# Hybrid encoder block on one core: gate of the product pairs one product later, dilated steps reordered, units run ahead

## The chip, the cores and the metric

The kernel runs on one core of a Trainium2 chip. The metric is the device time of one execution in microseconds; the median of the runs counts. The engines are named as the profile names them: PE (matrix engine; PEld is its weight load), DVE (vector), ACT (scalar), POOL (GpSimd) and SP (the sync engine, which here only issues DMAs). Each engine takes its instructions in the order in which the program wrote them to its queue, and each instruction waits until what it needs is done.

## The reference

One layer, one sequence of 1024 tokens of width 1024, float32. Three mixers run side by side on the normalised input: dilated window attention in three groups (A), grouped-query attention (B), and attention into a memory (M). Each is multiplied by a SiLU gate and projected; the three are merged by sigmoid gates and projected once more.

```python
h = rms_norm(x, g_pre)
a_qkv, bq, bk, bv, mq, ga, gb, gm, mg = split(h @ w_in)
aq, ak, av = rope(q of a_qkv), rope(k of a_qkv), v of a_qkv
for gi, (window, dil) in enumerate(((128, 1), (512, 4), (2048, 16))):      # 8 heads each, head size 64
    o_g, lse_g = dilated_window_attention(aq, ak, av of group gi, window, dil)
wts = softmax(stack(lses), axis=0)                                         # over the three groups
oa  = sum_g wts[g] * outs[g]
ob  = grouped-query attention of bq, bk, bv;   om = attention of mq into the memory
ya = (oa * silu(ga)) @ w_br_a;  yb = (ob * silu(gb)) @ w_br_b;  ym = (om * silu(gm)) @ w_br_m
gates  = sigmoid(mg + b_merge)
merged = gates[0] * ya + gates[1] * yb + gates[2] * ym
out = x + rms_norm(merged @ w_out, g_post)
```

## The kernel before

Every float32 matrix product is made of three products of a high and a low part (hh*wh, hl*wh, hh*wl); `split` makes the parts, ACT the high one (L105) and DVE the low one by a subtraction (L106). Nearly all the order after the grouped attention is written by hand: the text of the program is the order of each engine's queue.

**Start to 578.8 us.** Input norm, grouped attention, the projections that it needs, the values. The diff touches nothing here.

**The pairs (578.8 to 1081).** The remaining columns of the input projection are computed as 25 pairs of column blocks (`PAIRS`): in turn queries or keys that get their rotation ("rope"), and columns of the SiLU gates ("gate") or the merge gates ("merge"); the last is a merge pair. Each pair takes seven products of half size, after Strassen's scheme, of twelve matmuls each (`pair_product`, L1292), named A11, A12, S2, A22, S1, S3 and S4 by their operand. A product ends in a PSUM bank; `keep_copy` (ACT, L1296) copies some of them to SBUF, `c_add` adds two, and `c_fin` finishes a quarter of the result: a DVE multiplication by the row norm (L1098), then, in a merge pair, a tanh on ACT (L1106) and a store through ACT's own DMA queue into `thd` (L1107); in a gate pair a tanh (L1101), a DVE step and a store into `g2d` through SP. `k_block` splits the next operand, `turn_it` (POOL) rotates and `k_store` writes queries and keys.

**The turn (1081 to 1097).** `op_load`, `op_mult` and `op_split` fetch the first operand of the branch projections in two token halves (lo, hi), multiply it by its gate and split it into `hh` and `hl`.

**The dilated attention (1097 to 1300).** Twelve items, one for each pair of heads p (0 to 3) and group g (0 to 2), with eight steps T each. `plan` writes the order: in a step stand `trans` (PE turns the probabilities, DVE copies them out, L1555 and L1580), `soft` (DVE subtraction, ACT exponential L1542), a piece of the combination (`combining`), and loads or splits (`tokens`). `weave` puts between these steps, by costs, the pieces of a second stream: units 0 to 15 of the branch projections (`add_y`, L1815), 24 matmuls each, in two halves with a PSUM tile "d" of two buffers; `y_evac` empties one (DVE multiplies, L1344, POOL adds, L1345), `y_split` splits its weight, `y_load` and `th_load` fetch weight and merge gate.

`combine` joins the three groups of a head pair: fetch the statistics from memory (`cpt`, L1730), weights (DVE, from `cmn` L1735 to `ceg` L1746, with one ACT exponential L1739), write them to memory (put, L1751), read them back broadcast to the partitions (get, L1725), multiply and add the three outputs (`weigh`, L1760 and L1762; on POOL, for p = 3 the products on DVE), store. `STEP_T` gives the step of each piece. `b_load` and `b_split` fetch and split the grouped attention's output, the operand of units 8 to 15. `dl_load`, `dl_mult` (DVE, L1798) and `dl_split` fetch a combined head pair, multiply it by its gate and split it into `hh[k]`, `hl[k]`, the operand of units 16 to 23. All these loads are issued by SP.

**The ending (1300 to 1338).** After the last item, `ending` lists the pieces for p = 3 with their costs for `weave`.

**The y units 16 to 23 (1338 to 1382)**, `y_unit`, 24 matmuls each (L125), emptied whole (128x1024); between them stand the splits of the output weights (`LATER`) and of the merged result (`a_half`).

**The output projection (1382 to 1467)** and the final norm.

## Time and profile before

| | us |
|---|---|
| runs | 1469.06, 1469.36, 1475.54 |
| median | 1469.36 |
| profiled execution, its time | 1468.72 |
| its span in the trace | 1466.9 |
| PE busy | 1388.7 |
| DVE busy | 1028.3 |
| ACT busy | 659.9 |
| POOL busy | 600.4 |

How to read the lines that follow: in a timeline a line gives start, length, engine, source line of the program, operation, output<-input, shape and in brackets the idle time of the engine before the instruction and what ended it. In a table of waits a line gives engine, tile and line that waited, what it waited for, and then the microseconds in total, the number of times and the longest. In a table of windows each line gives the stretch, its length, the busy time of each engine, the granted clock of PE as a share of full speed, the busy share of the DMA engines and GB/s. SPq and ACTq are DMA issues on the queues of SP and ACT. Line numbers are those of the kernel before.

### The profile page before, as it was taken

What the parts mean: (1) busy time and instruction counts of PE and PEld (TensorE: products, weight loads), DVE (VectorE), ACT (ScalarE), POOL (GpSimd) and SP (SyncE); (2) the same over time, 40 slices, a digit from 0 to 9 for tenths busy, and PEclk for the clock granted to TensorE, in tenths of its full rate; (3) what the DMA queues carried; (4) which work ended last, traced back from release to release, by engine and by line L of the source; (5) the groups of instructions that cost most, each with busy time, mean ns of one, the idle gap of its engine ahead of it and who ended that gap; (6) DMA issues with size and microseconds to landing.
All of it is one profiled execution on the core that took longest, in us unless ns stands there. A gap on an engine that the chain in (4) does not pass through costs nothing.

```text
span 1466.9 us, 21800 instructions
## 1 busy us (share of the span) xinstructions
PE 1388.7 (95%) x7768; PEld 1109.3 (76%) x7768; DVE 1028.3 (70%) x1797; ACT 659.9 (45%) x1378; POOL 600.4 (41%) x455
## 2 busy tenths in 40 slices
PE   7999999999999999999999999999989899786997
PEld 7799986666666889887777788777767677565886
DVE  7768578677763987677766666677665655548977
ACT  6544366666554453333333333333346566432332
POOL 1416604676654002445455444555401325534303
PEclk9999999999999999999999999999999999888999
DMA  6347432232203795242333333333365667646454
GB/s 234 102 158 255 143 116 96 79 98 89 73 25 125 239 285 170 68 144 83 105 115 101 105 111 115 114 109 94 126 235 174 178 211 203 169 150 185 150 214 172
DMA packets 121341, 209.74 MB, mean 143 GB/s; under 512 B 33616, under 2 KB 62096, under 8 KB 121232
## 3 DMA queue, kind: packets, MB, share of 16 engines
q1 hardware_dynamic: 111920, 194.42, 41.5%
q10 hardware_dynamic: 9312, 13.93, 2.6%
q8 instruction: 61, 1.00, 0.3%
q14 instruction: 48, 0.39, 0.1%
HBM read 143.97 MB, written 64.32 MB: 142 GB/s over the span
## 4 chain that ended last, share of the span: by engine, by line
PE 70%; DVE 11%; issue 6%; ACT 4%; DMA 4%; POOL 3%; SPq 1%; ACTq 0%; DVEq 0%; POOLq 0%
PE s L1292 24%; PE s L1204 4%; PE s L1968 4%; PE ov L797 3%; PE sc L125 3%; PE s L1253 3%; PE d L145 3%; PE d L147 3%; PE d L143 3%; DVE vS L106 3%; PE s L782 2%; PE s L781 2%; PE tr L763 2%; PE d L1815 2%; PE tr L1601 2%
## 5 line engine op out<-in xcount | busy, mean ns | idle before, releaser
L788 POOL TENSOR_TENSOR bl<-bl,bp 128x512 f32<-128x512 f32 x96 | 130.9, 1363 | 54.2 <-ACT bp L784 48.8
L1292 PE MATMUL s<-hh,vS 128*128 128x512 f32 x400 | 134.6, 398 | 12.1 <-ACT vrt L1296 12.1
L1542 ACT ACTIVATE pra<-pra,sts 128x192 f32<-128x192 f32 (+2 forms) x192 | 81.2, 423 | 72.7 <-DVE sts L1541 71.8
L1292 PE MATMUL s<-vA,vS 128*128 128x512 f32 x450 | 109.6, 394 | 2.0 <-ACT vv L1296 2.0
L106 DVE TENSOR_TENSOR vS<-vot,vS 128x512 fp32r<-128x512 f32 x75 | 77.7, 1037 | 39.2 <-ACT vS L105 39.2
L1292 PEld LDWEIGHTS s<-vA,vS 128*128 128x128 f32 x450 | 83.6, 188 | 23.8 <-ACT vv L1296 6.1
L1292 PEld LDWEIGHTS s<-hh,vS 128*128 128x128 f32 x400 | 75.4, 189 | 33.6 <-ACT vrt L1296 16.4
L784 ACT ACTIVATE bp<-s 128x512 f32<-128x512 f32 x128 | 75.8, 596 | 43.2 <-PE s L782 42.2
L764 DVE TENSOR_REDUCE bn<-tr 128x1 f32<-128x512 f32 x128 | 84.8, 683 | 11.8 <-PE tr L763 10.7
L143 PE MATMUL d<-hh,wh 128*128 128x512 f32 x224 | 89.3, 399 | 2.4 <-DVE fth L216 2.4
L147 PE MATMUL d<-hh,wl 128*128 128x512 f32 x224 | 89.4, 399 | 0.0
L145 PE MATMUL d<-hl,wh 128*128 128x512 f32 x224 | 88.8, 397 | 0.0
L1292 PE MATMUL s<-hl,vS 128*128 128x512 f32 x200 | 79.0, 395 | 0.0
L1292 PE MATMUL s<-hh,wl 128*128 128x512 f32 x200 | 78.2, 391 | 0.0
L1292 PE MATMUL s<-hh,wh 128*128 128x512 f32 x200 | 78.2, 391 | 0.0
L1292 PE MATMUL s<-hl,wh 128*128 128x512 f32 x200 | 77.8, 389 | 0.0
L1327 POOL TENSOR_TENSOR wh<-wr,wh 128x512 fp32r<-128x512 f32 x16 | 21.9, 1369 | 110.8 <-ACT wh L1326 97.5
L1815 PE MATMUL d<-bh,wh 128*128 128x512 f32 x128 | 49.2, 444 | 17.9 <-DVE wl L1344 17.9
L1580 DVE COPY app<-tr 128x384 f32<-128x384 f32 (+1 forms) x64 | 38.7, 605 | 38.5 <-PE tr L1568 23.6
L1345 POOL TENSOR_TENSOR acc<-acc,wl 128x512 f32<-128x512 f32 (+1 forms) x23 | 42.1, 1833 | 44.7 <-DVE wl L1344 44.7
L797 PE MATMUL ov<-bp,VS 128*64 128x512 f32 x256 | 58.5, 598 | 0.0
L1044 POOL TENSOR_TENSOR vot<-vot,vA 128x512 f32<-128x512 f32 x12 | 19.0, 1586 | 92.1 <-DVE vS L106 92.1
(576 smaller groups left out, 4103.2 us busy)
## 6 DMA issues: line engine op xcount, KB each, us to landing
wr<-in_wu SPq DMA_DIRECT2D x40, 512.0 KB
vA<-in_wu SPq DMA_DIRECT2D x24, 512.0 KB
qkd<-ko SPq DMA_DIRECT2D x96, 128.0 KB
wl<-thd SPq DMA_DIRECT2D x24, 512.0 KB
wos<-os SPq DMA_DIRECT2D x12, 512.0 KB
aq<-qkd SPq DMA_DIRECT2D x12, 512.0 KB
ak<-qkd SPq DMA_DIRECT2D x12, 512.0 KB
wr<-in_wbr SPq DMA_DIRECT2D x24, 256.0 KB
```

Source lines behind the costliest of these rows:

```text
L106: V.tensor_tensor(dst_l, src, dst_h.bitcast(F32), op=OP.subtract)
L143: PE.matmul(dst, wh[:, k, :], hh[k][:, t], start=k == 0, stop=False)
L145: PE.matmul(dst, wh[:, k, :], hl[k][:, t], start=False, stop=False)
L147: PE.matmul(dst, wl[:, k, :], hh[k][:, t], start=False, stop=k == 7)
L764: fp["last"] = V.tensor_reduce(st[i]["n"][:, j, c:c + 1], s, axis=AX.X, op=OP.min)
L784: A.activation(pp, s, AF.Exp, scale=-1.0)
L788: G.tensor_tensor(lsum[i % 2], lsum[i % 2], pp, op=OP.add)
L797: PE.matmul(o[e * 64:e * 64 + 64], VS[:, kt, kv], d.pop(kt), start=kt < 2, stop=kt >= NT - 2)
L1204: PE.matmul(now[j], a, b, start=k == 0 and q == 0, stop=k == 3 and q == 2)
L1292: PE.matmul(BANK[n, c], a, b, start=k == 0 and q == 0 and not more, stop=k == 3 and q == 2, skip_group_check=c in "XW")
L1542: A.activation(src, src, AF.Exp, scale=-1.0, bias=bias, accum_out=sts[:, h, 1, T:T + 1])
L1815: PE.matmul(ps_, a, b, start=k == 0 and q == 0, stop=k == 3 and q == 2)
```

## The change

In the pairs, `c_fin` no longer issues the tanh and what follows it; it puts them in a list, and `behind()` issues them after the next product and its copy. `k_store` comes one product earlier. In the last pair the load of the hi half comes earlier, into other tiles, and is multiplied in four pieces.

In the dilated items, `soft` stands ahead of `trans` in each step. The combination has ten pieces at the steps 6, 7, 7, 0, 3, 3, 7, 4, 5 behind the fetch; the result is multiplied by its gate (`gate`) before it is stored, and its reload goes straight into `hl[k]`, without a multiplication. The split of a grouped-attention operand becomes ACT's half (`b_high`, T = 4) and DVE's half (`b_low`, T = 5).

For p = 3, the stores of the last statistics, fetch, put and get are issued by ACT instead of SP; the three outputs are gated first, and weighed in two halves on DVE; the loads of the output weights come behind. Of units 16 to 18 the products with head pairs 0 to 2 (`y_part`, k = 0 to 2) are put ahead of those with head pair 3; the splits of the output weights move to later units.

```diff
             if kind == "gate":
                 x = kr()
-                A.activation(x, r, AF.Tanh, scale=0.5)
-                V.scalar_tensor_tensor(r, x, 1.0, r, op0=OP.add, op1=OP.mult)
-                nc.sync.dma_start(g2d[GATES_P[u]][:, half[t]], r)
+
+                def gate_it():
+                    A.activation(x, r, AF.Tanh, scale=0.5)
+                    V.scalar_tensor_tensor(r, x, 1.0, r, op0=OP.add, op1=OP.mult)
+                    nc.sync.dma_start(g2d[GATES_P[u]][:, half[t]], r)
+                then.append(gate_it)
             else:
                 j = pairs[m][u]
-                A.activation(r, r, AF.Tanh, scale=0.5, bias=hbm[:, j:j + 1])
-                nc.scalar.dma_start(thd[j, :, half[t]], r)
+
+                def merge_it():
+                    A.activation(r, r, AF.Tanh, scale=0.5, bias=hbm[:, j:j + 1])
+                    nc.scalar.dma_start(thd[j, :, half[t]], r)
+                then.append(merge_it)
...
-            if k % 2 == 0:
-                OPM[t, k // 2] = vb.tile([P, 1024], F32, name=f"vA12{k // 2}")
-            for dst, src in ((OPM[t, k // 2], od), (tab[k // 2], g2d)):
-                nc.sync.dma_start(dst[:, half[k % 2]], src[2, k, :, t])
-
-    def op_mult(t):
-        for x in range(2):
-            V.scalar_tensor_tensor(OPM[t, x], OPM[t, x], 0.5, tab[x], op0=OP.mult, op1=OP.mult)
+            if t is lo and k % 2 == 0:
+                x = vb.tile([P, 1024], F32, name=f"vA12{k // 2}")
+                for z in range(2):
+                    OPM[lo, k + z] = x[:, half[z]]
+            elif t is hi:
+                OPM[hi, k] = kr()
+            for dst, src in ((tab[k // 2][:, half[k % 2]], g2d), (OPM[t, k], od)):
+                nc.sync.dma_start(dst, src[2, k, :, t])
+
+    def op_mult(t, k):
...
+    def behind():
+        while then:
+            then.pop(0)()
...
         pair_product(n, "S2")
         c_add(*((n - 1, 0, 1, BANK[n - 1, "W"], v_) if n else (0, 0, 0, BANK[0, "Y"], p1)))
+        behind()
...
-        if n > 1:
-            k_store(n - 2)
         if n == last:
+            op_load(hi)
             op_split(lo, 0)
             op_split(lo, 1)
...
         pair_product(*((N, "A11") if n < last else (n, "S4")))
         keep_copy(y_, n)
+        behind()
...
-    c_fin(last, 1, 0, BANK[last, "X"])
+        if n:
+            k_store(n - 1)
     for k in range(4):
         op_split(hi, k)
     r = RV[last, 0, 1]
     V.tensor_tensor(r, BANK[last, "Z"], r, op=OP.add)
+    c_fin(last, 1, 0, BANK[last, "X"])
     c_fin(last, 0, 1)
     c_fin(last, 1, 1)
+    behind()
...
+                E = nc.scalar if (p_, g) == (3, 2) else nc.sync
...
+                if it:
+                    out.append(it["soft"][T])
                 if T < LAG:
                     if pre:
                         out.append(pre["trans"][T + 8 - LAG])
                 elif it:
                     out.append(it["trans"][T - LAG])
-                if it:
-                    out.append(it["soft"][T])
...
-                if T == 5 and 1 <= n <= 5:
-                    if n > 1:
-                        b_split(n - 2)
-                    if n < 5:
+                if 1 <= n <= 5:
+                    if T == 4 and n > 1:
+                        b_high(n - 2)
+                    elif T == 5 and n > 1:
+                        b_low(n - 2)
+                    elif T == 6 and n < 5:
                         b_load(n - 1)
-                elif (n, T) in ((10, 4), (11, 4)):
-                    dl_load(n - 10)
-                    if n == 11:
-                        dl_gate(2, "q")
-                        dl_gate(3, "k")
-                elif (n, T) in ((10, 7), (11, 6)):
-                    dl_mult(n - 10)
-                elif (n, T) in ((11, 1), (11, 7)):
-                    dl_split(T // 7)
+                elif n in (9, 10):
+                    if T == 5:
+                        dl_load(n - 9)
+                elif n == 11:
+                    if T == 4:
+                        DL["g"] = qk.tile([P, S], F32, name="aq", bufs=2)
+                        nc.sync.dma_start(DL["g"], g2d[0, 3])
+                    for k in range(2):
+                        if T == k:
+                            dl_high(k)
+                        elif T == k + 1:
+                            dl_low(k)
+                    if T == 6:
+                        dl_high(2)
+                    elif T == 7:
+                        dl_low(2)
...
+            E = nc.sync if p_ < 3 else nc.scalar
...
-            def weigh(g):
-                wv = wgt[g].rearrange("p (b a) -> p a b", b=16)
-                ogv = ogs[g].rearrange("p (a b) -> p a b", b=16)
-                (G if p_ < 3 else V).tensor_tensor(ogv, ogv, wv, op=OP.mult)
+            def weigh(g, x=slice(0, 64), sums=None):
+                wv = wgt[g].rearrange("p (b a) -> p a b", b=16)[:, x]
+                ogv, og0 = [z.rearrange("p (a b) -> p a b", b=16)[:, x] for z in (ogs[g], ogs[0])]
+                (V if p_ == 3 else G).tensor_tensor(ogv, ogv, wv, op=OP.mult)
                 if g:
-                    G.tensor_tensor(ogs[0], ogs[0], ogs[g], op=OP.add)
+                    (V if p_ == 3 else G).tensor_tensor(og0, og0, ogv, op=OP.add)
+
+            def gate(g, gt):
+                V.scalar_tensor_tensor(ogs[g], ogs[g], 0.5, gt, op0=OP.mult, op1=OP.mult)
+
+            def load_gate():
+                c["g"] = cb.tile([P, S], F32, name="wgt", bufs=3)
+                nc.sync.dma_start(c["g"], g2d[0, p_])
 
             def store():
                 if p_ < 2:
...
                 else:
                     DL[p_] = ogs[0]
 
-            return [fetch, weights, put, get] + [lambda g=g: weigh(g) for g in range(3)] + [store]
+            if p_ == 3:
+                return dict(fetch=fetch, shares=shares, weights=weights, put=put, get=get, gate=gate, weigh=weigh)
+            return [fetch, shares, weights, put, get, lambda: weigh(0), lambda: [weigh(1), load_gate()], lambda: weigh(2),
...
+                    lambda: gate(0, c["g"]), store]
...
-        STEP_T = (7, 7, 7, 3, 3, 7, 2)
+        STEP_T = (6, 7, 7, 0, 3, 3, 7, 4, 5)
...
-        def b_split(k):
+        def b_high(k):
             h, l = [x[k] for x in OPER[1]]
-            split(h, l, l.bitcast(F32))
-
-        def dl_gate(k, x):
-            DG[k] = qk.tile([P, S], F32, name="a" + x, bufs=2)
-            nc.sync.dma_start(DG[k], g2d[0, k])
+            A.activation(h, l.bitcast(F32), AF.Copy)
+
+        def b_low(k):
+            h, l = [x[k] for x in OPER[1]]
+            V.tensor_tensor(l, l.bitcast(F32), h.bitcast(F32), op=OP.subtract)
...
         def dl_load(k):
-            DL[k] = qk.tile([P, S], F32, name="aq", bufs=2)
-            nc.sync.dma_start(DL[k], od[0, k])
-            dl_gate(k, "k")
-
-        def dl_mult(k):
-            V.scalar_tensor_tensor(DL[k], DL[k], 0.5, DG[k], op0=OP.mult, op1=OP.mult)
-
-        def dl_split(k, ts=(slice(0, S),)):
-            for t in ts:
-                split(hh[k][:, t], hl[k][:, t], DL[k][:, t])
+            nc.sync.dma_start(hl[k].bitcast(F32), od[0, k])
+            DL[k] = hl[k].bitcast(F32)
+
+        def dl_high(k, t=slice(0, S)):
+            A.activation(hh[k][:, t], DL[k][:, t], AF.Copy)
+
+        def dl_low(k, t=slice(0, S)):
+            V.tensor_tensor(hl[k][:, t], DL[k][:, t], hh[k][:, t].bitcast(F32), op=OP.subtract)
...
+            ogs = [OG.pop((3, x)) for x in range(3)]
+            com = combine(3, ogs)
+
+            DL[3] = ogs[0]
+
+            def weigh_half(x):
+                for g in range(3):
+                    com["weigh"](g, slice(32 * x, 32 * x + 32))
+
+            return [(com["fetch"], 100.0), (out_pool, 100.0), (lambda: [com["gate"](g, DL["g"]) for g in range(3)], 500.0),
+                    (com["shares"], 4000.0), (com["weights"], 2000.0), (com["put"], 0.0), (com["get"], 500.0),
+                    (lambda: weigh_half(0), 6000.0), (lambda: dl_high(3, lo), 500.0), (lambda: weigh_half(1), 100.0),
+                    (lambda: dl_low(3, lo), 500.0), (lambda: dl_high(3, hi), 500.0), (lambda: dl_low(3, hi), 500.0),
+                    (lambda: [wo_load(nm, k) for nm in ("B11", "B21") for k in range(4)], 500.0)]
...
+    def y_part(m, ks):
         n, i, f = steps[m]
-        wh, wl = YW.pop(m)
-        s = pss()
+        wh, wl = YW[m]
+        if m not in YP:
+            YP[m] = pss()
         for h in half:
-            terms = []
-            for k in range(4):
+            for k in ks:
                 gh, gl = [x[k][:, h] for x in OPER[i]]
-                terms += [(wh[:, k], gh), (wh[:, k], gl), (wl[:, k], gh)]
-            passes(s[:, int(h.start > 0)], terms)
-        return s
-
-    yp = None
-    LATER = {16: [("B21", 0), ("B21", 1)], 17: [("B21", 2), ("B21", 3)], 18: [("T2", 0), ("T1", 0)], 19: [("T2", 1), ("T1", 1)],
-             20: [("T2", 2)], 21: [("T2", 3)], 22: [("T1", 2)], 23: [("T1", 3)]}
+                for q, (a, b) in enumerate(((wh[:, k], gh), (wh[:, k], gl), (wl[:, k], gh))):
+                    PE.matmul(YP[m][:, int(h.start > 0)], a, b, start=k == 0 and q == 0, stop=k == 3 and q == 2)
+
+    LATER = {16: [("B11", 0), ("B11", 1)], 17: [("B11", 2), ("B11", 3)], 18: [("B21", 0), ("B21", 1)],
+             19: [("B21", 2), ("B21", 3), ("T2", 0), ("T1", 0)], 20: [("T2", 1), ("T1", 1)], 21: [("T2", 2)],
+             22: [("T2", 3), ("T1", 2)], 23: [("T1", 3)]}
+    y_split(17, G)
+    y_load(18)
+    ywp, yw = pool("yw", "right")
+    y_split(18, G, yw.tile([P, 1024], R, name="yw"))
+    y_load(19)
+    for m in range(16, 19):
+        y_part(m, range(3))
     for m in range(16, 24):
-        s = y_unit(m)
-        if yp:
-            y_evac(*yp)
-        yp = m, slice(0, S), s.rearrange("p a b -> p (a b)")
-        y_split(m + 1)
-        y_load(m + 2)
+        y_part(m, range(3, 4) if m < 19 else range(4))
+        if m > 16:
+            y_evac(m - 1, slice(0, S), YP[m - 1].rearrange("p a b -> p (a b)"))
+        if m in (16, 17):
+            y_split(m + 3, G)
+            y_load(m + 4)
+        elif m > 18:
```

More of the change, by code (lines that the diff above doesn't have):

```diff
@@ L1084, in kr @@
                 SPARE[z // 2 - 3][:, half[z % 2]])
-    RV, RP, RO = {}, {}, {}
+    RV, RP, RO, then = {}, {}, {}, []
     def c_add(n, u, t, ps_, z):
@@ L1392, in block @@
         c_fin(n, 0, 0)
+        if n == last:
+            for k in range(4):
+                op_mult(hi, k)
         pair_product(*((N, "A11") if n < last else (n, "S4")))
         keep_copy(y_, n)
+        behind()
         if n < last:
@@ L1405, in block @@
         c_add(n, 1, 1, BANK[n, "W"], y_)
+        behind()
         if n:
@@ L1415, in block @@
         if n == last - 1:
-            op_mult(lo)
+            for k in range(4):
+                op_mult(lo, k)
         pair_product(n, "S4")
         c_add(N, 0, 0, BANK[N, "Y"], p1)
+        behind()
         for nm in ("S1", "S3"):
@@ L1724, in load @@
                 for h in range(2):
-                    nc.sync.dma_start(wgt[g][h * 64:h * 64 + 64], wgd[p_, h, g:g + 1].to_broadcast([64, S]))
+                    E.dma_start(wgt[g][h * 64:h * 64 + 64], wgd[p_, h, g:g + 1].to_broadcast([64, S]))
             def fetch():
@@ L1736, in weights @@
                 V.tensor_tensor(mn, mn, cpt[:, 2, 0], op=OP.min)
-                eg = cb.tile([P, 3, 16], F32, name="ceg", bufs=1)
+                c["e"] = eg = cb.tile([P, 3, 16], F32, name="ceg", bufs=1)
                 V.tensor_tensor(eg, cpt[:, :, 0], mn[:, None, :].to_broadcast([P, 3, 16]), op=OP.subtract)
                 A.activation(eg, eg, AF.Exp, scale=-1.0)
+            def weights():
+                cpt, eg = c["t"], c["e"]
                 dn = cb.tile([P, 3, 16], F32, name="cdn", bufs=1)
```

50 lines of the change are left out of this document (22 added, 28 removed).

## The prediction

> **What bounds the kernel now.** I read the page's first block, then the busy time of each engine by stage, then what the matrix engine waits for in each stage, and last the timeline around each wait.
>
> ```profile
> PE 1388.7 (95%) x7768; PEld 1109.3 (76%) x7768; DVE 1028.3 (70%) x1797; ACT 659.9 (45%) x1378; POOL 600.4 (41%) x455
> ```
> ```profile
> core 0: us, PE busy (x) PEld busy (x) DVE busy (x) ACT busy (x) POOL busy (x), PEclk, DMA share, GB/s
> 578.80:1081.00 502.20, 488.09 (x2094) 393.04 (x2094) 352.07 (x383) 175.42 (x278) 244.82 (x145) 1.00 0.35 111
> 1097.00:1240.00 143.00, 131.54 (x1388) 106.32 (x1389) 85.98 (x384) 89.33 (x325) 40.97 (x21) 0.98 0.63 192
> 1338.00:1382.00 44.00, 43.73 (x192) 35.89 (x193) 43.62 (x37) 15.60 (x29) 22.91 (x10) 1.00 0.56 190
> 1382.00:1467.00 85.00, 77.09 (x348) 63.42 (x346) 66.87 (x107) 26.37 (x61) 13.21 (x22) 0.97 0.49 174
> ```
>
> PE is busy 1388.7 of 1466.9 us, and the change takes no matmul away: what can be won is its idle time and the slow matmuls after long idle. In the pair stage (578.8 to 1081) 14.1 us are idle; in the y units at 1338 to 1382 both PE (43.73 of 44) and DVE (43.62 of 44) are full, so that stage is the one to watch for a loss.
>
> **A. The pairs: gate one product later.** These two lines are all of PE's waits there, and the timeline (start, length, engine, line) shows one of them:
>
> ```profile
> PE s L1292 <- ACT vrt L1296: 12.1, 8, 1.6
> PE s L1292 <- ACT vv L1296: 2.0, 1, 2.0
> ```
> ```profile
> 691.38 0.68 DVE L1098 TENSOR_TENSOR vv<-vv,rb 128x512 f32<-128x512 f32 x1
> 692.09 0.72 ACT L1106 ACTIVATE vv<-vv,hbm 128x512 f32<-128x512 f32 x1 [5.09 <-DVE vv L1098]
> 693.22 0.60 ACT L1296 ACTIVATE vrt<-s 128x512 f32<-128x512 f32 x1 [0.40 <-ACT vv L1106]
> 693.87 0.50 PE L1292 MATMUL s<-hh,vS 128*128 128x512 f32 x1 [1.58 <-ACT vrt L1296]
> ```
>
> ACT reaches the tanh of L1106 at its place in its queue, sits 5.09 us idle until DVE has multiplied (L1098), and only then copies the product out of PSUM (L1296), for which PE waits. The change puts the tanh and its store (for the sigmoid pairs also the DVE step and SP's store) behind the next copy. ACT's idle 5.09 us then hold the copy. The copied product is the last but one that PE ran; one is 12 matmuls (2.7 us at 488.09/2094 = 0.23) and PE stopped at 693.87 - 1.58 = 692.29, so it had ended near 689.6, and its copy can be done near 690.3, 2 us ahead of need. All nine waits have this form, so 14.1 us go. What becomes late instead is the tanh, by the copy's 0.60; behind it on ACT stands the next operand's split, on DVE (352 of 502 us busy) the second gate step, on SP and ACT the stores, whose readers come much later. I leave 1 us for a wait that reappears: **-13**, between 0 (the next operand is as late) and -14.1.
>
> **B. The turn from the pairs.** The last head pair's gating is now loaded and multiplied earlier, and its split stands ahead of the last tanh.
>
> ```profile
> 1087.86 0.50 PE L1815 MATMUL d<-hh,wh 128*128 128x512 f32 x1 [2.51 <-ACT hh L105]
> PE s L1529 <- DVE vy L1427: 0.6, 1, 0.6
> ```
>
> The loads go out about a product and a half earlier, so both waits (the add of L1427 now stands behind the splits on DVE, which works against the second) should go: 3.1 us; I take **-3**, between 0 and -3.1.
>
> **C. The dilated items, head pairs 0 to 2.**
>
> ```profile
> PE tr L1601 <- DVE app L1580: 5.5, 2, 2.8
> PE tr L1594 <- DVE app L1555: 2.8, 2, 1.6
> DVE bl L106 <- ACT bh L105: 7.2, 4, 2.0
> DVE cmn L1735 <- DMA cpt<-std: 3.4, 2, 3.2
> ```
>
> PE's first two waits are 8.3 us, in four places where DVE in turn sits 7.2 us behind ACT's copy bh: the split of an attention operand whose halves stood together. The change puts ACT's half a step ahead of DVE's, so about 7 of the 8.3 go, if ACT is not late by a whole step: -5.5 to -8.3. Softmax ahead of the turning of probabilities in each step may be worth 1 us either way; I take -1. Against it stands the combination: its first minimum (cmn) moves from T=7 to T=6, a step nearer to the fetch of cpt. DVE waits there 3.4 us at two places already; twelve items of eight steps lie between 1097 and 1300, 2.1 us a step, so at three places it waits up to 2 us more, half of which reaches PE. Taken: -6 -1 +3 = **-4**, between -9 and +3.
>
> **D. The gating of finished head pairs.** Today a finished pair is reloaded with its gate and multiplied on DVE.
>
> ```profile
> 1277.39 1.23 DVE L1798 SCALAR_TENSOR_TENSOR aq<-aq,ak 128x1024 f32<-128x1024 f32 x1 [8.90 <-issue]
> 1295.24 1.23 DVE L1798 SCALAR_TENSOR_TENSOR aq<-aq,ak 128x1024 f32<-128x1024 f32 x1 [5.71 <-DMA ak<-g2d]
> PE tr L1614 <- DVE app L1580: 6.0, 1, 6.0
> PE d L1815 <- DVE wl L1344: 3.8, 1, 3.8
> ```
> ```profile
> 1279.20:1284.00 4.80, 4.44 (x18) 3.12 (x20) 3.16 (x16) 3.47 (x13) 1.52 (x1) 0.50 0.29 62
> 1297.10:1302.00 4.90, 4.46 (x12) 3.06 (x13) 2.41 (x7) 3.38 (x8) 2.79 (x3) 0.50 0.48 146
> ```
>
> DVE stops 8.90 and 5.71 us ahead of the two multiplies, PE 6.0 and 3.8 us behind them, and the two windows right after show PE granted half its clock, which makes 4.7 us of matmuls out of some 2.4 each time: 9.8 + 4.5 = 14.3. In the changed kernel the multiply is done on the combined result before it is stored, and the reload goes into the operand's own buffer at item 9 and 10, whole items ahead of its split at item 11. Both stops lose their cause. The clock rule of the Trainium skill ("TensorE: Matmul & The Clock Gate", What's actually happening: after an idle window of about 3.4 us the clock is halved until about 3.4 us of work have passed) agrees with these 3.8 and 6.0 us gaps; by it the slow matmuls go with the gaps. New waits: SP's load of the gate stands behind POOL's first weighing, and the gate's multiply on DVE waits for POOL's last; I leave 2 us. **-12.5**, between -8 and -14.3.
>
> Front: -13 -3 -4 -12.5 = **-32.5** (about -20 to -41).
>
> **E. The end: last head pair by ACT's queue, units run ahead.**
>
> ```profile
> 1302.99 0.59 SPq L1730 DMA_DIRECT2D cpt<-std  x1
> 1305.25 1.07 ACT L1609 ACTIVATE og<-tr 128x512 f32<-128x512 f32 x1 [4.51 <-PE tr L1594]
> 1312.40 1.27 SPq L1751 DMA_DIRECT2D wgd<-ceg  x2
> 1317.12 3.99 SPq L1725 DMA_DIRECT2D wgt<-wgd  x6
> 1320.50 7.90 DMA wgt<-wgd
> 1323.75 1.91 DVE L1760 TENSOR_TENSOR og<-og,wgt 128x1024 f32<-128x1024 f32 x1 [10.13 <-DMA wgt<-wgd]
> 1328.49 3.60 DVE L1760 TENSOR_TENSOR og<-og,wgt 128x1024 f32<-128x1024 f32 x1 [0.57 <-DMA wgt<-wgd]
> 1332.01 0.68 DVE L1344 SCALAR_TENSOR_TENSOR wl<-wl,d 128x512 f32<-128x512 f32 x1
> 1332.75 0.80 PE L1815 MATMUL d<-bh,wh 128*128 128x512 f32 x1 [13.88 <-DVE wl L1344]
> 1337.31 0.40 PE L125 MATMUL sc<-hh,wh 128*128 128x512 f32 x1
> ```
>
> The weights go to memory (put, 1312.40) and come back widened (get, 1317.12, landing at 1320.50 + 7.90 = 1328.4, called T). The wait is a round trip of DMAs, and PE idles 13.88 us because unit 15 needs a "d" buffer that DVE frees only behind the weighing.
>
> What the other queue gives: between put and get SP issued 3.45 us of other loads, which now come after; but on ACT the fetch stands behind the copy of the last attention output (L1609, done at 1306.32), 3.3 us later. With fewer transfers beside it I put T 1.4 us earlier against the last statistics (+-2.5). The Trainium skill ("DMA: Bandwidth & Descriptors", Issuing engines are not separate DMA queues) says that DMAs of any issuer share the same engines and another issuer saves only issue time; by it T would gain nothing but these 3.45 us, and less after the later fetch.
>
> What the run-ahead gives: units 16 to 18 may multiply three of four head pairs before T, 54 matmuls, 54 x 43.73/192 = 12.3 us. But in the changed program's queue of PE they stand behind units 14 and 15. The "d" tiles have two buffers; unit 15's first half waits for the emptying of unit 14's, and DVE's queue has that behind both halves of the weighing. So PE stops at unit 15 as before, and the 54 come after the wait, not in it. Behind T, DVE does the rest: a half multiply is 1.91/2 = 0.96, a half add 0.68; one multiply and add of the first half, four of the second, the low half of the split and the emptying, 7.3 us in all (4.35 before: 1332.75 - 1328.4). Then PE has 24 + 54 + 6 matmuls until unit 16 is complete: 84 x 0.228 = 19.1, and about 1.8 for the slow clock (12 matmuls took 1332.75 to 1337.31 where 2.7 would do): T + 28.2.
>
> ```profile
> 1361.59 1.21 DVE L1344 SCALAR_TENSOR_TENSOR wl<-wl,sc 128x1024 f32<-128x1024 f32 x1
> 1362.87 2.79 POOL L1345 TENSOR_TENSOR acc<-acc,wl 128x1024 f32<-128x1024 f32 x1 [2.36 <-DVE wl L1344]
> 1363.32 2.88 DVE L106 TENSOR_TENSOR wT<-wT 128x512 fp32r<-128x512 f32 x1
> 1366.13 0.68 DVE L1881 SCALAR_TENSOR_TENSOR aq<-acc,aq 128x512 fp32r<-128x512 f32 x1
> 1366.73 1.21 DVE L1344 SCALAR_TENSOR_TENSOR wl<-wl,sc 128x1024 f32<-128x1024 f32 x1
> ```
>
> DVE's first emptying of these units (L1344) follows at T + 29.5; it was at T + 17.8 (1361.59 and 1366.73 are the fourth and fifth, so the first was near 1346.2). From there DVE has its own pace. One period is 5.14 us with three operations between emptyings, one of which always falls on POOL's add and takes 2.88 where the same shape takes 0.68; so a period with n of them is 1.13 + 2.8 + 0.6 (n - 1). The changed order has 2, 2, 5, 4, 3, 3, 2 between the eight emptyings: 4.5 + 4.5 + 6.3 + 5.7 + 5.1 + 5.1 + 4.5 = 35.9, as long as before (7 x 5.14). PE's finished matmuls wait beside it. So the last unit comes 11.7 later against T, less the 1.4 of T, less about 1.5 that the output projection (77.09 busy of 85) takes up in its own gaps: **+8.8**, from -6.5 (rival 1) to +14 (T later by 2.5, no gap used). If the batch of PE were DVE's cover instead, PE alone gives 84 + 120 matmuls or T + 55, +2 against before: that end is inside.
>
> **The sum.** Span 1466.9 - 32.5 + 8.8 = 1443.2. The profiled execution's time, 1468.72, is 1.8 above its span, and the median of the runs (1469.36) 0.6 above that: 1445.6, forecast **1445** against 1469.36.
>
> **The rivals.**
> 1. *The run-ahead covers the wait.* If unit 15 gets its buffers before T, the 54 matmuls fill PE's 13.9 us, unit 16 needs six more, DVE empties at about T + 11.4 and the end moves by 11.4 - 17.8 - 1.4 = -7.8, less what the projection waits for else: -6.5. Time 1445.6 - 15.3 = **1430**. Against it: both queues' order and the two buffers. Chance 0.12.
> 2. *The pairs gain nothing:* with the copy early, PE waits as long for the operand split that stands behind the moved tanh on ACT. For it: the tanh cannot start before 692.09, and ACT has it all to do after. Against: ACT's 175 busy of 502 us. 1445.6 + 13 = **1459**. Chance 0.08.
> 3. *Slower: DVE is what is late in the front.* It is busy 70% there, in order, and each wait that I remove stood ahead of it; the new gates (1.2 us each on DVE, ahead of softmax) and the halves could stall it in the same items, on POOL's weighing, which takes the DMA's place. All of the front's 32.5 then return, and the end's 8.8 stay: **1478**. It decides from the point where 31 of the 32.5 come back; below 17 the kernel is still faster. Against: PE's waits in A are behind ACT alone, not DVE. Chance 0.09.
> 4. *Every DVE operation beside POOL is slowed, not one per add.* 14 further ones between the emptyings at 2.2 us more: +31, **1476**, no change. The row says one per period. The Trainium skill ("SBUF — State Buffer", Who interferes with whom) holds that a DVE instruction with two SBUF inputs and a reading GpSimd instruction lock each other out for the whole instruction; that is the 2.88 beside 2.79, and it ends with POOL's one add. Chance 0.05.
>
> **How the numbers follow.** The forecast has 0.66, its own range 1432 to 1458. Range 1427 to 1464: it takes in rivals 1 and 2 and leaves out 3 and 4 and the tails. 0.5%, 7.3 us, is about what a measurement of this kernel can tell from no change. Faster (below 1462.0): 0.66 + 0.12 + 0.08, less 0.02 for the tail: 0.84. Same: 0.05 + 0.02 = 0.07. Slower: 0.09.
>
> **What would show it.** PE's waits of the pairs for L1296 gone, the tanh's idle on ACT now ahead of the copy's successor; no stop of DVE at L1798's place; the wait for bh gone; T about 27 us behind the last statistics; PE stopped for over 8 us at unit 15, then 78 matmuls in a row; the emptyings of units 16 to 23 some 5 us apart and ending about 65 us behind T. Wrong if PE runs L125's successors inside the wait (rival 1), if waits for a vS or wh operand of like size appear in the pairs (2), or if DVE's idle in items 3 to 11 is behind POOL (3).

## The result, and the profile after

| | us |
|---|---|
| before, median of 20 runs | 1469.66 (1467.68 to 1475.54) |
| changed, median of 20 runs | 1467.17 (1465.14 to 1470.99) |
| ratio changed to before | 0.9976, interval 0.9967 to 0.9986 |
| forecast | 1445 (1427 to 1464) |
| profiled execution of the changed kernel, its span | 1464.3 |

The kernel got 2.5 us faster, a quarter of a percent: a gain clear of noise, but a tenth of the forecast 24 us. One execution behind the times below was slow (1720 us, of the run with the old steps); it is left out of that run's median, which is that of the other three. It is not that the edits did little. The same events in both traces show what was won and given back:

| event | before | changed | moved by | so this stretch | forecast |
|---|---|---|---|---|---|
| last matmul of the pairs starts | 1082.22 | 1061.58 | -20.6 | -20.6 | -13 |
| first statistics of the dilated items | 1109.29 | 1096.61 | -12.7 | **+8.0** | -3 |
| statistics of the tenth item | 1255.89 | 1246.45 | -9.4 | **+3.2** | -4 |
| statistics of the twelfth item | 1300.04 | 1279.23 | -20.8 | -11.4 | -12.5 |
| last weights land (T) | 1328.40 | 1311.65 | -16.8 | **+4.1** | -1.4 |
| first emptying of units 16 to 23 | 1346.18 | 1343.36 | -2.8 | **+13.9** | +11.7 |
| last emptying | 1382.02 | 1379.29 | -2.7 | +0.1 | 0 |
| end of the span | 1466.9 | 1464.3 | -2.6 | +0.1 | -1.5 |

In the first stretch 0.6 us of the 20.6 are there already when the pairs begin. The page's first block and the windows (length, busy time of PE, PEld, DVE, ACT, POOL, then PE's clock, DMA share, GB/s) of the changed kernel:

```profile
PE 1386.2 (95%) x7768; PEld 1113.6 (76%) x7768; DVE 1034.6 (71%) x1805; ACT 659.7 (45%) x1377; POOL 601.3 (41%) x457
```
```profile
578.80:1081.00 502.20, 494.59 (x2146) 401.93 (x2145) 363.94 (x409) 182.35 (x290) 245.57 (x147) 1.00 0.38 120
1300.00:1338.00 38.00, 18.86 (x76) 15.34 (x77) 12.48 (x16) 3.58 (x6) 10.49 (x8) 0.71 0.49 149
```

PE's totals differ by 2.5 us; the reader who stops there learns nothing. The second window does tell: at 1300 to 1338, which unit 15 and the run-ahead are meant to fill, PE is busy for half the time, at a clock of 0.71.

### The profile page after: what moved, and what is told of

It is laid out like the page before. It is cut to its first block, busy times and chain, and to the rows that moved or that the text cites. A ratio compares the mean times of both kernels' runs of the same rounds, so it can differ in the third digit from the quotient of the medians.

```text
span 1464.3 us, 21835 instructions
## 1 busy us (share of the span) xinstructions
PE 1386.2 (95%) x7768; PEld 1113.6 (76%) x7768; DVE 1034.6 (71%) x1805; ACT 659.7 (45%) x1377; POOL 601.3 (41%) x457
## 4 chain that ended last, share of the span: by engine, by line
PE 75%; DVE 6%; DMA 6%; POOL 5%; issue 3%; ACT 2%; SPq 2%; DVEq 0%; ACTq 0%; POOLq 0%
PE s L1298 32%; PE s L1210 4%; PE s L2030 4%; PE ov L797 3%; PE s L1259 3%; PE d L145 3%; PE d L143 3%; PE d L147 3%; PE d L1859 2%; PE s L782 2%; PE s L781 2%; PE tr L763 2%; PE d L2030 1%; DMA wgt<-wgd 1%; PE d L538 1%
## 5 line engine op out<-in xcount | busy, mean ns | idle before, releaser
L1298 PE MATMUL s<-vA,vS 128*128 128x512 f32 x450 | 106.6, 390 | 0.0
L106 DVE TENSOR_TENSOR vS<-vot,vS 128x512 fp32r<-128x512 f32 x75 | 85.6, 1143 | 19.9 <-ACT vS L105 19.9
L1336 POOL TENSOR_TENSOR wh<-wr,wh 128x512 fp32r<-128x512 f32 x19 | 26.6, 1401 | 132.6 <-ACT wh L1335 132.6
L1564 DVE CUSTOM_DVE_ANT_0 pra<-s,mask 128x192 f32<-128x192 f32 (+2 forms) x192 | 54.6, 323 | 37.1 <-PE s L1552 17.7
L1302 ACT ACTIVATE vv<-s 128x512 f32<-128x512 f32 x50 | 30.0, 599 | 86.0 <-PE s L1298 58.1
```

Source lines behind the costliest of these rows:

```text
L106: V.tensor_tensor(dst_l, src, dst_h.bitcast(F32), op=OP.subtract)
L1298: PE.matmul(BANK[n, c], a, b, start=k == 0 and q == 0 and not more, stop=k == 3 and q == 2, skip_group_check=c in "XW")
```

## The experiments

Each time stands against the kernel before run beside it on the same chip (medians 1469.85, 1470.72 and 1469.34 in the three sets).

| run | us | against before | interval of the ratio |
|---|---|---|---|
| weighing behind units 14, 15 | 1455.91 | -13.9 | 0.9887 to 0.9916 |
| loads of output weights early | 1462.24 | -7.6 | 0.9931 to 0.9964 |
| first unit's weight first | 1465.94 | -3.9 | 0.9952 to 0.9977 |
| later tanh only | 1451.32 | -18.5 | 0.9854 to 0.9889 |
| old steps | 1460.94 | -9.8 | 0.9912 to 0.9946 |
| old turn | 1463.14 | -7.6 | 0.9931 to 0.9960 |
| last head pair on SP | 1456.95 | -13.8 | 0.9890 to 0.9923 |
| units 16, 17 ahead, old turn | 1442.07 | -28.7 | 0.9788 to 0.9817 |
| the same, SP, old steps | 1435.77 | -33.6 | 0.9738 to 0.9794 |
| the same, half a weighing sooner | 1432.72 | **-36.6** | 0.9714 to 0.9776 |
| changed, but tanh at its old place | 1482.16 | +12.8 | 1.0051 to 1.0106 |

**The pairs alone.** The kernel before, with the list and `behind()` of the change and nothing else:

```diff
-                A.activation(r, r, AF.Tanh, scale=0.5, bias=hbm[:, j:j + 1])
-                nc.scalar.dma_start(thd[j, :, half[t]], r)
+                def merge_it():
+                    A.activation(r, r, AF.Tanh, scale=0.5, bias=hbm[:, j:j + 1])
+                    nc.scalar.dma_start(thd[j, :, half[t]], r)
+                then.append(merge_it)
...
         keep_copy(y_, n)
+        behind()
```

> The kernel before with one part of the change: tanh and what follows it in a pair are issued behind the next product's copy, all else as before. Theory: the pairs gain what PE's weight loads waited (22.5 us in the row of PEld), not only what PE itself waited (14.1 us): the stage is 19 to 21 us shorter, and the kernel takes 1448 to 1452. Rival: the gain is 14, the rest came from the other parts: 1454 to 1457; or the turn gives most of it back as it did in the changed kernel: 1458 to 1463.

1451.32: this one part is worth 18.5 us, seven times the whole change. Waits of the weight loads (PEld) in the pairs of the kernel before, and the window of the pairs in this run:

```profile
PEld s L1292 <- ACT vrt L1296: 16.4, 11, 2.0
PEld s L1292 <- ACT vv L1296: 6.1, 11, 2.4
```
```profile
578.80:1064.00 485.20, 485.20 (x2112) 396.22 (x2111) 357.05 (x386) 178.29 (x281) 244.30 (x145) 1.00 0.37 116
```

PE's own row showed nine stops, 14.1 us. PEld's show 22 stops, 22.5 us: in 13 of them the weight load waited while PE still ran matmuls already loaded, which PE's row books as busy. By the starts of its matmuls, PE lost 19.9 us in the stage (what lies between two starts beyond the usual 0.23 us, summed). After the edit PE is busy for every microsecond of the stage.

**The change without it.** The converse, the changed kernel with the tanh at its old place:

```diff
-                then.append(gate_it)
+                gate_it()
...
-                then.append(merge_it)
+                merge_it()
```

> The changed kernel with the tanh and what follows it issued at their old place in the pairs, all else as changed. Theory: the later tanh alone gave 18.5 us in the kernel before, and the other parts together cost 16: without it the changed kernel is slower than the kernel before, 1481 to 1487. Rival: the later tanh is itself what makes the turn late (SP's loads wait for the stores of ACT's queue), so without it the turn is shorter and the loss smaller: 1473 to 1480.

1482.16, in the theory's interval: the other parts together cost 12.8 us, where the forecast had them at about -11. The two parts alone add up to -5.7, the whole change gave -2.5; so 3.2 us of the loss belong to their meeting, and most of it to the other parts by themselves. But the rival's mechanism is there too. From the last matmul of the pairs to the first statistics it is 26.8 us here (1082.84 to 1109.65), as in the kernel before (27.1), where the changed kernel has 35.0.

**The turn.** In the changed kernel, in order: what SP waited for, the chain, ACT and PE:

```profile
SPq L1318 <- DMA thd<-vy: 6.5, 1, 6.5
```
```profile
1052.64 4.05 DMA thd<-vy
...
1058.59 7.49 DMA wr<-in_wbr
```
```profile
1066.10 0.63 ACT L1335 ACTIVATE wh<-wr 128x512 fp32r<-128x512 f32 x1 [8.20 <-DMA wr<-in_wbr]
1066.79 0.80 PE L1859 MATMUL d<-hh,wh 128*128 128x512 f32 x1 [4.81 <-ACT wh L1335]
```

SP stands at a load of the hi half's gate until a store of the merge gate, issued by ACT, has landed; the load of unit 0's weight (`wr`, L1330) is behind it, goes out at 1058.59 and lands at 1066.08, when the pairs had been over for 4 us. The splits of the hi half stand on ACT behind that weight's split. The load has no use for that store; but in the trace's records it waits, before it is issued, for semaphore 109, the one that this store raises when it has landed, and raises the same one itself. The slow clock behind the stop counts as well: from the last matmul of the pairs to the first statistics PE is busy 27.4 us for 23.5 before, at a granted clock of 0.85 for 1.00, and idle 7.6 for 3.6. I read the cause as the order of loads on SP and put the weight first:

```diff
         if n == last:
+            y_load(0)
             op_load(hi)
...
             qk_first(0)
-            y_load(0)
             th_load(0)
```

> The changed kernel with the load of the first unit's weight (y_load(0)) ahead of the load of the operand's hi half at the last pair. Theory: the turn from the pairs lost about 11 us against the forecast because this load stood behind the hi half's fourth piece, which SP issued 6.5 us late behind a store of ACT's queue, so it landed at 1066 when the pairs had ended at 1062, PE idle 4.8 us and then on half clock. With it ahead, the first unit starts at the end of the pairs, and the kernel takes 1460 to 1463. Rival: the next late thing (the merge gate's load, for which DVE waits 5.3 us until 1079.3, or the hi half's splits) stands right behind and PE waits there instead: 1465 to 1468.

1465.94, the rival's. Unit 0 began without a wait (1063.11), but in this order the hi half is late: DVE waits 3.03 us for one piece, PE 2.18 us behind it, and the turn takes 32.5 us.

```profile
1062.66 0.69 DVE L1321 SCALAR_TENSOR_TENSOR vy<-vy,tab 128x512 f32<-128x512 f32 x1 [3.03 <-DMA vy<-od]
1065.92 0.73 PE L1859 MATMUL d<-hh,wh 128*128 128x512 f32 x2 [2.18 <-DVE wh L1336]
```

Then the old turn as a whole, with the later tanh: `k_store` and the last pair's loads, `op_mult` and finishes as before.

```diff
-            op_load(hi)
             op_split(lo, 0)
             op_split(lo, 1)
...
             y_load(0)
+            op_load(hi)
```

> The changed kernel with the turn from the pairs as before: the loads of the operand's hi half, their two multiplications and the order of the last finishes are those of the kernel before; the tanh stays behind the next copy. Theory: this turn, not the later tanh itself, costs the 8 us between the last product of the pairs and the first statistics (34.6 us for 26.8): they come back, 1458 to 1462. Rival: the first statistics come sooner, but the items behind wait for the same loads and give it back: 1464 to 1468.

1463.14, between the two expectations. The turn takes 28.8 us, 6.2 less than in the changed kernel's profile. So it is the two parts together: the new turn with the old tanh 26.8, the old turn with the new tanh 28.7 to 29.6 (five profiles), both 32.0 to 35.0 (four profiles of that same stretch of program). The forecast booked both as gains, each by itself. SP's stop is there with the old tanh too (the run with the tanh at its old place):

```profile
SPq L1318 <- DMA thd<-vy: 6.8, 1, 6.8
```

But there the weight goes out 5.9 us before the last matmul of the pairs starts, in the changed kernel 3.0, and PE waits 0.37 us for it instead of 4.81: the later tanh moved the store, and all that stands behind it on SP, nearer to the end of the pairs.

**The items.** DVE and ACT waits of the changed kernel between 1097 and 1280, and ACT's second one before:

```profile
DVE cmn L1769 <- DMA cpt<-std: 8.6, 3, 4.1
ACT og L1632 <- POOL og L1798: 9.4, 3, 4.2
```
```profile
ACT og L1609 <- POOL og L1762: 1.4, 1, 1.4
```

The first stood at 3.4 us before and was forecast to grow. The second was not in the forecast: the get, a step later, makes POOL's weighing later, POOL frees the output buffers later, and ACT's copies (L1632) stand in order in front of the exponentials.

```diff
-        STEP_T = (6, 7, 7, 0, 3, 3, 7, 4, 5)
+        STEP_T = (7, 7, 7, 7, 3, 3, 7, 4, 5)
```

> The changed kernel with the steps of the combination as near as may be to those before: (7, 7, 7, 7, 3, 3, 7, 4, 5) for (6, 7, 7, 0, 3, 3, 7, 4, 5), so the first minimum stands a step further from its fetch, and the get directly behind the put. Theory: items 2 to 9 lost 3 us instead of gaining 4 because DVE waits 8.6 us for the fetched statistics (3.4 before) and ACT's copies of the attention output wait 9.4 us for POOL's weighing (1.4 before), PE behind both for some 7 us. Then these two waits fall to about 4 and 2 us, and the kernel takes 1461 to 1465. Rival: these waits lie beside other work of PE, or the earlier get holds SP's queue at the put and the loads behind it come late: 1466 to 1470.

1460.94, at the lower edge of the theory's interval: two numbers of the list are worth about 7 us. Which of the two waits they end is to be read from the last two versions below, which have the same steps; the first of them between 1097 and 1280:

```profile
DVE cmn L1763 <- DMA cpt<-std: 5.8, 3, 5.2
ACT og L1626 <- POOL og L1792: 1.6, 1, 1.6
```

In the second of them the two stand at 8.7 and 2.4 us; in the run with units 16 and 17 ahead, which has the other steps, at 8.3 and 10.9. So the wait behind POOL is what the earlier get ended; DVE's wait for the statistics hardly fell, against the theory, and the stretch from the first statistics to the tenth is shorter all the same (143.6 and 144.8 us for 149.8).

**The other queue.** ACT's queue in the changed kernel, then the chain:

```profile
1290.97 1.27 ACTq L1787 DMA_DIRECT2D wgd<-ceg  x2
1292.89 11.78 ACTq L1759 DMA_DIRECT2D wgt<-wgd  x6
```
```profile
1294.26 9.30 DMA wB<-wod
1303.56 0.02 issue
1303.58 0.45 ACTq L1759
1304.03 0.04 issue
1304.07 7.58 DMA wgt<-wgd
```

The six issues of the get, 3.99 us on SP before, take 11.78: the fourth goes out at 1299.83 and the fifth at 1303.58, 20 ns after a load of output weights, issued meanwhile by SP, has landed. The records of the trace name what they wait for: SP's and ACT's DMAs raise eight completion semaphores in all, both queues use each of them, and the fifth issue waits for number 100, which that load raises. So a get waits here for a load that it has nothing to do with, and which the old order kept behind it. Where SP's loads come later (the run with units 16 and 17 ahead), the same six issues on ACT's queue are short:

```profile
1290.95 3.78 ACTq L1753 DMA_DIRECT2D wgt<-wgd  x6
```

Two runs took either the queue or the loads out of the way:

```diff
-                E = nc.scalar if (p_, g) == (3, 2) else nc.sync
+                E = nc.sync
...
-            E = nc.sync if p_ < 3 else nc.scalar
+            E = nc.sync
```

> The changed kernel with the DMAs of the last head pair issued by SP, as before, instead of ACT. Theory: ACT's queue is no gain here; the get stood 11.8 us at its six issues behind loads that SP issued meanwhile, and the fetch behind the copy of the last output. On SP the fetch comes sooner by about 3 us and the get's six issues take 4 us, so T comes 4 to 8 us sooner: 1459 to 1463. Rival: put and get now stand behind the loads of weight and merge gate on SP, which the change moved ahead, and T is as late: 1465 to 1469.

```profile
1290.12 3.87 SPq L1759 DMA_DIRECT2D wgt<-wgd  x6
```
```profile
1293.54 5.69 DMA wgt<-wgd
...
1306.65 8.02 PE d L1859 x24
```

1456.95, 11.3 better than the changed kernel against the same kernel before, more than expected: T is 23.2 us behind the last statistics (1276.02 to 1299.23), 32.4 in the changed kernel. (Another 3.1 us between the two profiles lie in the turn, which the edit does not touch.) And the loads issued ahead instead:

```diff
-            return [(com["fetch"], 100.0), (out_pool, 100.0), ...
+            return [(com["fetch"], 100.0), (out_pool, 100.0),
+                    (lambda: [wo_load(nm, k) for nm in ("B11", "B21") for k in range(4)], 100.0), ...
...
-                    (lambda: [wo_load(nm, k) for nm in ("B11", "B21") for k in range(4)], 500.0)]
```

> The changed kernel with the eight loads of the output weights B11 and B21 issued right behind the fetch of the statistics instead of at the end of the list. Theory: the get of the last head pair, now on ACT's queue, is held at its 4th and 5th issue (1299.8 and 1303.6 in the trace of the changed kernel) until loads of these weights, issued meanwhile by SP, have landed, because an issue waits for the end of an earlier DMA of the other queue; with those loads ahead and mostly done, the six issues take about 4 us and T comes 4 to 7 us sooner against the put: 1460 to 1463. Rival: the gets are slow because the transfers share the DMA engines' bandwidth, and a load ahead delays fetch, put and get as much as a load beside: 1466 to 1470.

1462.24, the expected time by half the expected way: the six issues still took 7.16 us and began 3.7 us behind the put (1.9 in the changed kernel). The put itself took 3.59 us to land there, 1.90 in the run on SP's queue: that speaks for transfers in each other's way, the rival's reason, but no run shows it alone. The third weighing began at 1307.31 where it was 1311.74.

**The run-ahead.** The wait and what follows it in the changed kernel; in the chain, the matmuls of units 15 and 16 to 18:

```profile
1318.32 0.68 DVE L1353 SCALAR_TENSOR_TENSOR wl<-wl,d 128x512 f32<-128x512 f32 x1
1319.14 0.76 PE L1859 MATMUL d<-bh,wh 128*128 128x512 f32 x1 [24.50 <-DVE wl L1353]
1343.36 1.21 DVE L1353 SCALAR_TENSOR_TENSOR wl<-wl,sc 128x1024 f32<-128x1024 f32 x1
1379.29 1.21 DVE L1353 SCALAR_TENSOR_TENSOR wl<-wl,sc 128x1024 f32<-128x1024 f32 x1
```
```profile
1319.14 7.30 PE d L1859 x24
1326.45 14.99 PE sc L1944 x66
```

As forecast, PE stops at unit 15 and then runs the units in a batch. One number moves DVE's emptying of 14 and 15 ahead of the weighing:

```diff
-                    (lambda: weigh_half(0), 6000.0), ...
+                    (lambda: weigh_half(0), 26000.0), ...
```

> The changed kernel with one cost of the weave raised (weigh_half(0) 6000 to 26000), so that on DVE the emptying of units 14 and of half of unit 15 stands ahead of the weighing of the last head pair. Theory: the run-ahead of units 16 to 18 is lost because unit 15 stands ahead of it on PE and waits for a buffer that DVE frees behind the weighing (PE idle 24.5 us). Then PE runs units 14, 15 and the 54 matmuls inside the wait, unit 16 is complete about 9 us behind the landing T of the weights instead of 31, and the kernel takes 1444 to 1452 us (15 to 23 less than the changed kernel's 1467). Rival: the last stage is held by DVE's own chain of emptyings and splits, whatever PE does ahead: 1463 to 1468.

1455.91, 11.4 better than the changed kernel, less than the theory's 15 to 23: unit 15 and unit 16 ran in the wait, but unit 17 not, whose weight split stood on ACT behind the split that waits for the weighing. The lines are PE's wait ahead of unit 17 and the first emptying:

```profile
1316.52 0.79 PE L1944 MATMUL sc<-hh,wh 128*128 128x512 f32 x1 [4.36 <-ACT wh L1335]
1333.98 1.21 DVE L1353 SCALAR_TENSOR_TENSOR wl<-wl,sc 128x1024 f32<-128x1024 f32 x1
```

So that split was moved ahead too, with two units instead of three and the old turn:

```diff
+                    (lambda: [y_split(17, G), y_load(18)], 26000.0),
                     (lambda: weigh_half(0), 6000.0), ...
...
-    for m in range(16, 19):
+    for m in range(16, 18):
         y_part(m, range(3))
```

> Three edits together: the turn as before, the weighing behind the emptying of units 14 and 15, and the weight split of unit 17 ahead of ACT's split of the weighed pair, with two units (16 and 17, not 18) run ahead. Theory: in the run with the weighing moved alone the run-ahead was still cut, because the weight split of unit 17 stood on ACT behind the split that waits for the weighing (PE idle 4.4 us, then 2.1), and unit 16 was complete only when 17 and 18 had run. Now PE has 36 matmuls inside the wait and completes unit 16 first, 10 to 14 us sooner than in that run (1455.9), and the turn gives about 7 us more: 1434 to 1441. Rival: DVE's chain from unit 16 on sets the end and starts hardly sooner, since the splits of the output weights wait for their loads: 1446 to 1451, the turn's part alone.

1442.07, a microsecond outside the theory's interval. The first emptying stands at 1319.46.

**Together.** To that, SP's queue and the old steps:

> The three edits of the run with units 16 and 17 ahead and the old turn (1442.1), and besides the last head pair's DMAs on SP and the steps of the combination (7, 7, 7, 7, 3, 3, 7, 4, 5). Theory: the parts add up where they lie in different stages: the steps give 5 to 6 us, as they gave alone. SP's queue gave 10 us alone, but most of it was the get held behind the loads of the output weights, which here are issued later anyway, and DVE starts the weighing only behind the emptying of unit 15; so it gives 0 to 3: 1433 to 1438. Rival: the parts overlap wholly (a sooner T ends in the same batch of PE, which is busy without a gap from 1300 on): 1440 to 1443.

1435.77, in the theory's interval. And half a weighing ahead of unit 15's emptying on DVE, by the costs in another order:

```diff
-                    (lambda: [y_split(17, G), y_load(18)], 26000.0),
-                    (lambda: weigh_half(0), 6000.0), ...
+                    (lambda: weigh_half(0), 14000.0),
+                    (lambda: [y_split(17, G), y_load(18)], 18000.0), ...
```

> As the run beside it, but the first half of the weighing stands ahead of the emptying of unit 15 on DVE (costs 14000 and 18000 for 26000 and 6000 in another order). Theory: the weighing no longer starts behind unit 15's matmuls, PE has units 15, 16 and 17 to run meanwhile, and unit 16 is complete 2 to 4 us sooner: 1430 to 1436, 1 to 4 below the run beside it. Rival: from unit 16 on PE and DVE are both full and the splits of the output weights, whose loads are no sooner, hold the first emptying: no more than 1 us between the two runs.

1432.72, the best version: 36.6 us below the kernel before. The 3 us against the run beside it are not clear of noise (four executions each, 1431.58 to 1434.35 and 1433.65 to 1438.35). Its first emptying, 43.7 us behind the last statistics, where the run beside it has 44.9:

```profile
1312.35 1.21 DVE L1350 SCALAR_TENSOR_TENSOR wl<-wl,sc 128x1024 f32<-128x1024 f32 x1
```

## Why the prediction was wrong, point by point

**The sum's mistakes** are 7.6 us too careful in the pairs, and too hopeful by 11.0 in the turn, 7.2 from the first statistics to the tenth, 1.1 in the gating, 5.5 at T, 2.2 in the batch and 1.7 behind it: 21.1 net.

**A, -13: right mechanism, mis-sized.** All of PE's waits for the copy went, as worked out. The term was taken from PE's waits (14.1) where the stops of its weight loads (22.5), or the starts of its matmuls (19.9), were the better measure; -20 was measured in the trace, -18.5 in the run alone.

**B, -3: wrong sign.** The step that failed is "the loads go out about a product and a half earlier, so both waits should go". They did go out earlier, and took the place ahead of the first unit's weight, in a queue that stood for 6.5 us behind ACT's store; PE stopped for 4.81 us and then ran at a lower clock. I had looked for what the moved loads gain and not for what they push back on SP, nor at the store that the same change made later.

**C, -4: wrong sign.** The split of the operands did what it should: DVE's wait for it fell from 7.2 to 0.4 us. The combination took 5.2 more at cmn, which I had bounded rightly (up to 2 at three places); and it added 8.0 at the copies behind POOL, a consequence of the later get that I did not follow through POOL's queue. That is the step that failed: the term of the combination (+3) was priced at cmn alone. With the old steps the copies' wait is down to 1.6 and 2.4 us, the one at cmn stays. My upper bound, +3, is about what came.

```profile
DVE bl L1836 <- ACT bh L1832: 0.4, 1, 0.4
```

**D, -12.5: right**, -11.4. Both stops are gone from items 11 and 12; from the tenth statistics to the twelfth PE is idle 3.6 us for 12.1, at a clock of 0.94 for 0.83. Where C ends and D begins is uncertain by some 3 us: in eight profiles with these steps the stretch up to the tenth statistics takes 146.6 to 150.3 us, but from the first to the twelfth all have 182.4 to 184.8, for 190.8 before. With the old steps it is 175.8 and 177.1: -15.0 and -13.6, near the -16.5 forecast for C and D together.

**E, +8.8: right in sign and mechanism, 9.4 too small.** PE resumed 7.5 us behind T (7.3 worked out) and had unit 16 complete by T + 28.6 (28.2), the emptyings took 35.9 us from first to last (35.9 worked out), and the first came at T + 31.7 (29.5), behind two splits of output weights that took DVE 1.97 us. The 1.5 us that the output projection was to take up did not come (+0.1). The Trainium skill ("SBUF — State Buffer", Who interferes with whom) agrees with the pace: one DVE operation in each period is locked out by POOL's add (2.90 us for 0.68, beside an add of 2.79), and only one. What failed is "I put T 1.4 us earlier": it was 4.1 later, because the other queue was not free of SP's loads. The Trainium skill's rule ("DMA: Bandwidth & Descriptors", Issuing engines are not separate DMA queues), that another issuer saves issue time alone, was the better guide, and the runs went beyond it: here the other issuer cost 9.2 us of T.

**The rivals.** The run-ahead did not cover the wait (rival 1); it does when two orders are mended, and the first of them alone gave 11.4 of the 15.3 us that this rival had. The pairs gained in full (2 wrong). DVE was not what was late in the front (3 wrong), but its general form, gains coming back as waits in other stages, is what happened, for about 15 us: at a DMA queue and at POOL, where I had looked at DVE. The range ended at 1464, short of no change, and three terms came out beyond their own bounds: A at -20 (bound -14.1), B at +8.0 (bound 0), E at +18.2 (bound +14). The bounds of each part had been set from the kernel before alone, as if one part's new lateness could not meet another part's. The gain that came lies inside the 0.5% that the prediction counted as no change, to which it had given 0.07.

**Left open:** neither late tanh nor new turn alone makes the turn long, and SP's stop behind ACT's store is where they meet; but no run took the shared semaphore alone away, so what the turn would be without that stop is not shown. The same stretch of program varied between 32.0 and 35.0 us over four profiles. How much of the loss in the items is DVE's wait for the statistics stays open too.

## What to carry to other kernels

Read the weight loads' row of waits as well as the matmuls': a stop that the pipeline hides once shows there and adds up. When a change moves a DMA to another queue, or ahead in one, write down what is behind it on that queue and which earlier transfers its issue waits for; here two queues that share completion semaphores were one queue at the worst moment. And measure the parts of a change alone as well as together, above all where one makes a transfer later and the other depends on transfers: one part alone was worth seven times the whole. The best version here keeps the later tanh, the gating and the split operands, mends the run-ahead, and takes back the turn, the queue and two of the steps.

## What the runs showed of the hardware that was not expected

An issue on ACT's queue came 3.75 us behind the one ahead of it (1299.83 to 1303.58), with nothing to wait for but an unrelated load of SP's; by the trace's records the two share completion semaphore 100. The other way round, a load of SP's stood for 6.5 us until an unrelated store of ACT's had landed, and the two share number 109. And a PE that is booked as busy 488.09 of 502.2 us could be made 20 us faster without a matmul less.
